# Gate/up groups of a hybrid decoder layer: the second weight block added by transfers onto two others, products in another order, and k tiles 8 to 11 by seven products

## The chip, the cores and the metric

The kernel runs on one core of one Trainium2 chip. The metric is the device time of one execution in microseconds (us); three runs of the kernel before have a median of 1966.47 us (1966.36 to 1967.82).

## The reference

One decoder layer on 256 tokens with D_MODEL 2048 and D_FF 5632, all in float32: a SwiGLU feed-forward half step with LayerNorm, a token mixer (latent attention beside differential attention, merged by sigmoid gates) with LayerNorm, and a second feed-forward half step with LayerNorm.

```python
def _swiglu(x, w_gate, w_up, w_down):
    return (jax.nn.silu(x @ w_gate) * (x @ w_up)) @ w_down

def reference(...):
    h = _layer_norm(ALPHA * h + 0.5 * _swiglu(h, ffn1_w_gate[l], ffn1_w_up[l], ffn1_w_down[l]), ...)
    mix = _mixer(h, ...)          # h @ w_in, two attentions, gates, w_out
    h = _layer_norm(ALPHA * h + mix, ...)
    h = _layer_norm(ALPHA * h + 0.5 * _swiglu(h, ffn2_w_gate[l], ffn2_w_up[l], ffn2_w_down[l]), ...)
```

## The kernel before

**Products in three parts.** Every float32 matmul is made of three matmuls on rounded operands (`triple`, L207 to L210): high part of x by high part of the weight (L208), high by low (L209), low by high (L210). A weight tile must therefore be split on the core first (`split`, L152 to L156): ScalarE (ACT) casts the raw tile to its high part (L154), VectorE (DVE) subtracts that from the raw tile to make the low part (L155). Both parts go into a ring of six pairs, `wring`.

**Units.** Work on weights is cut into units of two k tiles (a k tile is 128 rows of the weight) by 512 columns, one 128x1024 tile of 512 KB. `advance` (L173) runs three stages per unit in program order: `load` (a transfer issued by SP, three units ahead), `prep` (adds and split, four units ahead of the products) and `now` (the matmuls). A plain unit serves both blocks of 128 tokens: 2 k tiles x 2 token blocks x 3 = 12 matmuls of 512 columns.

**Gate/up by seven products.** `Hybrid.group` (L383 on) takes two neighbouring 512-column weights w0 and w1 together. For the k tiles that it handles this way the weight is a 2 by 2 matrix of blocks, "11" and "21" from w0, "12" and "22" from w1 (upper and lower k tiles), and the tokens' matrix is one of 2 by 2 blocks as well, so seven products do in place of eight (Strassen's scheme, in the form of Winograd). Products 1, 5, 6, 7, 2, 4, 3 run on sums of blocks: 1 on 11; 5 on 11+12; 6 on 11+12+22; 7 on 12+22; 2 on 21; 4 on 11+12+22+21; 3 on 22. The sums are made in place in the raw tiles `R[...]` before they are split. The tokens' sums are made once per layer part (`Seven` for k tiles 0 to 7, `Extra` for the others). The remaining k tiles are plain units, `p` on w0 and `q` on w1. PSUM banks X, Y, Z and W gather the products, and `done` subtracts or adds saved copies (`snaps`) and applies SwiGLU (gus L940, hb L921; transposed at L717 and sent out in 8 transfers at L719).

Each feed-forward part has a first pair of weights by `project` and ten groups, p = 1 to 10. Groups 2 to 9 are wide: their seven products cover k tiles 0 to 7 in two 128x1024 tiles per block (s = 0, 1) and k tiles 8 and 9 in one 128x512 tile per block (s = 2, `eraw`); k tiles 10 to 15 are three plain units on each weight. So a wide group has 7 x (6 + 6 + 3) = 105 matmuls by seven products and 6 x 12 = 72 plain ones, 177 in all. Groups 1 and 10 and six groups of the mixer (three for gates, wdq, wdk, wdv) are narrow: two tiles per block and 4 + 4 plain units.

**What sets the order.** The order of a group is a string, one character per product or plain unit: "15pp6p72q4q3q" for a wide group. Every engine executes its instructions in the order in which they were recorded, and `split_in_line` and `behind_split` tie the order of splits and adds on DVE. In a wide group three of the four sums are made by DVE (L430: 11 += 12 before product 5, 11 += 22 before 6, 11 += 21 before 4, each two adds of 128x1024 and one of 128x512). The fourth, 12 += 22 for product 7, is made by transfers that POOL issues (L432): each reads block 22 from memory once more and accumulates it onto 12 in place. In the mixer's groups DVE makes all four.

The blocks are loaded at L422, the plain units at L459.

## Time and profile before

| | |
|---|---|
| median of three runs | 1966.47 us (1966.36 to 1967.82) |
| the profiled execution, first to last instruction | 1963.9 us |
| what lies around that span, against the median | 2.6 us |
| TensorE (PE) busy | 1952.0 us, 99% |
| DVE busy | 1779.9 us, 91% |
| ACT busy | 1251.5 us, 64% |
| POOL busy | 312.1 us, 16% |
| mean granted TensorE clock | 0.998 |

The profile is of one execution. Its page gives busy times, the chain of work that ended last, groups of instructions and transfers; its trace answers for stretches of time, for the instructions of one engine in order of time, and for what an engine waited for. Busy times of neighbouring instructions on one engine overlap by some tens of ns, so the pitch from one start to the next says more than a duration.

### The profile page before, as it was taken

To read this page: it belongs to the slowest core of one execution; us is meant where nothing else is said; L and a number is where in the kernel's file an instruction comes from. 1 tells how busy PE (TensorE), PEld (TensorE's weight loads), DVE (VectorE), ACT (ScalarE), POOL (GpSimd) and SP (SyncE) were. 2 spreads that over 40 slices of the span, in tenths; PEclk is the share of its full clock that TensorE was granted. 3 is DMA by queue.
4 is the path that set the end of the run, shared out by engine and by line. 5 is a ranking of instruction groups with operands and counts; after the bars stand their busy time and mean duration, and the time that the engine had idled before them with its cause. 6 is when DMAs were issued, how large, how long until landed. Compare 5 with 4: busy or idle time off the path is not lost.

```text
span 1963.9 us, 25802 instructions
## 1 busy us (share of the span) xinstructions
PE 1952.0 (99%) x8763; PEld 1617.7 (82%) x8763; DVE 1779.9 (91%) x2189; ACT 1251.5 (64%) x1640; POOL 312.1 (16%) x536
## 2 busy tenths in 40 slices
PE   9999999999999999999999999999999999999998
PEld 7888888888888898888788888888888888888886
DVE  7999999999998879988987777789999999999997
ACT  6666766676655566666667655556676666665662
POOL 0112111122100010102241530001211112210000
PEclk9999999999999999999999999999999999999999
DMA  8978888878776667767685798587888878787773
GB/s 314 289 225 262 270 260 249 257 233 300 272 235 222 210 216 258 239 223 252 211 254 195 237 305 271 201 264 254 252 269 263 250 240 277 241 318 236 277 232 124
DMA packets 150228, 488.86 MB, mean 249 GB/s; under 512 B 21792, under 2 KB 22096, under 8 KB 150096
## 3 DMA queue, kind: packets, MB, share of 16 engines
q1 hardware_dynamic: 119232, 401.00, 59.7%
q0 software_dynamic: 30720, 86.09, 16.8%
q8 instruction: 68, 1.11, 0.2%
q14 instruction: 64, 0.52, 0.1%
q10 hardware_dynamic: 144, 0.13, 0.0%
HBM read 456.73 MB, written 30.41 MB: 248 GB/s over the span
## 4 chain that ended last, share of the span: by engine, by line
PE 95%; DVE 2%; DMA 1%; issue 1%; ACT 0%; POOL 0%; SPq 0%; DVEq 0%; ACTq 0%; POOLq 0%
PE mm L208 30%; PE mm L210 30%; PE mm L209 30%; DVE wring L155 1%; PE tr L208 1%; PE tr L210 1%; PE tr L209 1%; PE tr L673 0%; DMA turned<-turn 0%; ACT wring L154 0%; DMA sraw<-in_wdk_dram 0%; DVE sraw L430 0%; PE tr L1376 0%; PE tr L1304 0%; PE tr L1378 0%
## 5 line engine op out<-in xcount | busy, mean ns | idle before, releaser
L154 ACT CAST wring<-raw 128x1024 fp32r<-128x1024 f32 (+2 forms) x468 | 482.7, 1035 | 323.5 <-PE mm L210 237.6
L155 DVE TENSOR_TENSOR wring<-raw,wring 128x1024 fp32r<-128x1024 f32 (+2 forms) x468 | 557.0, 1198 | 95.6 <-ACT wring L154 93.5
L154 ACT CAST wring<-sraw 128x1024 fp32r<-128x1024 f32 x436 | 453.1, 1052 | 201.7 <-DVE sraw L430 83.6
L155 DVE TENSOR_TENSOR wring<-sraw,wring 128x1024 fp32r<-128x1024 f32 x436 | 520.3, 1218 | 20.6 <-ACT wring L154 17.8
L208 PE MATMUL mm<-wring,h 128*128 128x512 f32 (+2 forms) x1248 | 480.9, 385 | 0.1
L210 PE MATMUL mm<-wring,h 128*128 128x512 f32 (+2 forms) x1248 | 480.3, 385 | 0.0
L209 PE MATMUL mm<-wring,h 128*128 128x512 f32 (+2 forms) x1248 | 479.9, 385 | 0.0
L208 PE MATMUL mm<-wring,xs 128*128 128x512 f32 x776 | 302.2, 389 | 0.5 <-ACT snap L387 0.5
L209 PE MATMUL mm<-wring,xs 128*128 128x512 f32 x776 | 302.1, 389 | 0.0
L210 PE MATMUL mm<-wring,xs 128*128 128x512 f32 x776 | 301.9, 389 | 0.0
L210 PEld LDWEIGHTS mm<-wring,h 128*128 128x128 f32 x1248 | 234.4, 188 | 47.0 <-DVE h L155 0.7
L208 PEld LDWEIGHTS mm<-wring,h 128*128 128x128 f32 x1248 | 234.4, 188 | 46.7 <-ACT h L154 0.6
L209 PEld LDWEIGHTS mm<-wring,h 128*128 128x128 f32 x1248 | 234.4, 188 | 46.1
L430 DVE TENSOR_TENSOR sraw<-sraw,sraw 128x1024 f32<-128x1024 f32 x168 | 199.1, 1217 | 2.0 <-DMA sraw<-in_wdk_dram 1.6
L208 PEld LDWEIGHTS mm<-wring,xs 128*128 128x128 f32 x776 | 145.6, 188 | 31.0 <-ACT snap L387 0.9
L209 PEld LDWEIGHTS mm<-wring,xs 128*128 128x128 f32 x776 | 145.7, 188 | 30.5 <-DVE wring L155 0.3
L210 PEld LDWEIGHTS mm<-wring,xs 128*128 128x128 f32 x776 | 145.7, 188 | 30.2
L719 POOL DMA_DIRECT2D hT<-blocks x176 | 96.8, 563 | 368.3 <-DVE blocks L717 367.2
L209 PE MATMUL mm<-wring,x 128*128 128x512 f32 x336 | 130.9, 390 | 0.2 <-DVE wring L155 0.2
L208 PE MATMUL mm<-wring,x 128*128 128x512 f32 x336 | 130.1, 390 | 0.8 <-ACT wring L154 0.8
L210 PE MATMUL mm<-wring,x 128*128 128x512 f32 x336 | 130.7, 389 | 0.0
L432 POOL DMA_DIRECT2D sraw<-in_gu_dram x40 | 35.6, 892 | 371.4 <-DVE sraw L430 334.5
(328 smaller groups left out, 2292.4 us busy)
## 6 DMA issues: line engine op xcount, KB each, us to landing
sraw<-in_gu_dram SPq DMA_DIRECT2D x160, 512.0 KB, 5.2
raw<-in_gu_dram SPq DMA_DIRECT2D x158, 512.0 KB, 5.0
raw<-in_dn_dram SPq DMA_DIRECT2D x140, 512.0 KB, 4.7
sraw<-in_gu_dram POOLq DMA_DIRECT2D x40, 512.0 KB, 7.5
sraw<-in_dn_dram SPq DMA_DIRECT2D x36, 512.0 KB, 5.4
eraw<-in_gu_dram SPq DMA_DIRECT2D x64, 256.0 KB, 5.8
raw<-in_w_out_dram SPq DMA_DIRECT2D x32, 512.0 KB, 4.3
hraw<-hT POOLq DMA_DIRECT2D x56, 256.0 KB, 5.9
```

Source lines behind the costliest of these rows:

```text
L154: cast[0] = S.copy(hi, src)
L155: lows[0] = V.tensor_tensor(out=lo, in0=src, in1=hi.bitcast(F32), op=ALU.subtract)
L208: PE.matmul(o, xh, wh, start=first, stop=False, skip_group_check=again)
L209: PE.matmul(o, xh, wl, start=False, stop=False, skip_group_check=again)
L210: PE.matmul(o, xl, wh, start=False, stop=last, skip_group_check=again)
L430: last = V.tensor_tensor(out=R[src][i], in0=R[src][i], in1=R[add[1]][i], op=ALU.add)
L432: nc.gpsimd.dma_start(R["12"][s], source("22", s), accum_op=ALU.add)
L719: nc.gpsimd.dma_start(to.rearrange("(g r) (i f) -> i r g f", g=4, i=4)[i], t[32 * i:32 * (i + 1), :].rearrange("r (g f) -> r g f", g=4))
```

## The change

Block 12 is not loaded by itself any more. In every group transfers issued by POOL read it from memory and accumulate it in place onto block 11, once product 1 has been split from that, and onto block 22, once product 6's sum has been made from it (`added = {1: "11", 6: "22"}`, L436). DVE keeps two sums of each group: 11 += 22 for product 6 (L431), and 21 += 11 for product 4 (L439), made right behind the split of product 2 from the same tile.

The order of products changes to "15p36p27qn4q" for a wide group, and `Hybrid.run` records all groups of a part as one sequence: at the character n it emits product 1 of the next group, ahead of this group's product 4 and last q.

`Extra` now takes k tiles 8 to 11 by seven products (full 128x1024 tiles with s = 2), so a wide group has two plain units p and two q: 7 x 18 + 4 x 12 = 174 matmuls. Bank Z comes from the other PSUM pool. Lines move: the loads stand at L423 and L463, gus at L944, hb at L925, the transpose at L721 and its transfers at L723.

```diff
-            f = tmp_tile([P, 2, 2, P], "fe")
-            fa, fb = f[:, 0], f[:, 1]
+            a0, a1, c0, c1 = (raw[:, b, i * 256:(i + 1) * 256] for i in range(2) for b in range(2))
+            fa, fb = (tmp_tile([P, 2, 256], "fe") for _ in range(2))
             for out, in0, in1 in ((fa[:, 0], a1, c1), (fb[:, 0], a1, a0), (fa[:, 1], a0, fa[:, 0]), (fb[:, 1], c0, fa[:, 1])):
                 V.tensor_tensor(out=out, in0=in0, in1=in1, op=ALU.subtract)
-            t = act_tile([P, 2, 2, 2, P], F32R, "xe")
...
                 for m, p in enumerate(pair):
-                    self.at_[p] = [t[:, w, i, m] for w in range(2)]
-            k = 4 * self.q
+                    self.at_[p] = [t[:, w, m].rearrange("p (k t) -> p k t", k=2) for w in range(2)]
             for b, p in enumerate((2, 4)):
-                self.at_[p] = [self.x.at(w, k + 1, b) for w in range(2)]
...
@@ -356,22 +355,27 @@
...
             self.raws = {n: early[n] if n in early else [act_tile([P, 1024], F32, "sraw") for _ in range(2)]
-                         for n in ("11", "12", "22")}
-            self.raws["21"] = [act_tile([P, 1024], F32, "sraw") for _ in range(2)]
-            self.shared = False
+                         for n in ("11", "22", "21")}
             if extra is not None:
-                for pair in (("11", "12"), ("22", "21")):
-                    t = act_tile([P, 2, 512], F32, "eraw")
-                    for i, n in enumerate(pair):
-                        self.raws[n] = self.raws[n] + [t[:, i, :]]
+                for n in self.raws:
+                    self.raws[n] = self.raws[n] + [act_tile([P, 1024], F32, "sraw")]
...
+        def run(self, groups):
+
+            parts = [self.group(*g[:-1]) for g in groups]
+            for i, (order, emit) in enumerate(parts):
+                if groups[i][-1] is not None:
+                    groups[i][-1]()
+                for c in order if i == 0 else order[1:]:
+                    if c != "n":
+                        emit(c)
+                    elif i + 1 < len(parts):
+                        parts[i + 1][1]("1")
...
@@ -381,9 +385,10 @@
...
-            plan = {1: ("11", "11", None, "X"), 5: ("12", "11", ("11", "12"), "Z"), 6: ("22", "11", ("11", "22"), "X"),
-                    7: (None, "12", ("12", "22"), "X"), 2: ("21", "21", None, "Y"), 4: (None, "11", ("11", "21"), "W"),
-                    3: (None, "22", None, "Z")}
+            plan = {1: ("11", "11", None, "X"), 5: (None, "11", None, "Z"), 3: ("22", "22", None, "Z"),
+                    6: (None, "11", "22", "X"), 7: (None, "22", None, "X"), 2: ("21", "21", None, "Y"),
+                    4: (None, "21", None, "W")}
+            added = {1: "11", 6: "22"}
...
-                    banks[n] = mm_bank()
+                    banks[n] = tr_bank() if n == "Z" else mm_bank()
...
@@ -406,15 +411,11 @@
 
             def source(name, s):
                 w, j0 = blocks[name]
-                if s < 2:
-                    return w[j0 + s]
-                i = j0 // 2
-                return w[4][:, i * 512:(i + 1) * 512]
+                return w[j0 + s if s < 2 else 4 + j0 // 2]
...
                     last = None
-                    if add is not None and (small or p != 7):
+                    if add is not None:
                         for i in {0: (0,), 1: tuple(range(1, end_s + 1)), 2: ()}[s]:
                             with nullcontext() if small else behind_split(s + 1):
-                                last = V.tensor_tensor(out=R[src][i], in0=R[src][i], in1=R[add[1]][i], op=ALU.add)
-                    if not small and p == 6:
-                        nc.gpsimd.dma_start(R["12"][s], source("22", s), accum_op=ALU.add)
-                    pair = [v[:, :tiles * 512] for v in next_pair()]
+                                last = V.tensor_tensor(out=R[src][i], in0=R[src][i], in1=R[add][i], op=ALU.add)
+                    pair = next_pair()
                     with tc.issue_after(last.ins) if last is not None and not small else nullcontext():
                         split_in_line(not small, *pair, t)
-                    st["pair"] = [v.rearrange("p (g n) -> p g n", g=tiles) for v in pair]
+                    if p in added:
+                        nc.gpsimd.dma_start(R[added[p]][s], source("12", s), accum_op=ALU.add)
+                    elif p == 2:
+                        with nullcontext() if small else behind_split(1):
+                            V.tensor_tensor(out=t, in0=t, in1=R["11"][s], op=ALU.add)
+                    st["pair"] = [v.rearrange("p (g n) -> p g n", g=G) for v in pair]
...
-                    for g in range(tiles):
+                    for g in range(G):
                         if s < 2:
                             xh, xl = (v[:, 2 * s + g, :] for v in self.seven.at_[p])
                         else:
-                            xh, xl = self.extra.at_[p]
+                            xh, xl = (v[:, g, :] for v in self.extra.at_[p])
...
             end = self.k_tiles // G - 1
-            if self.shared:
-                order = "15pp6p7p3q2q4qq" if seeded else "1p5p6p7p3q2q4qq"
-            elif wide:
-                order = "15pp6p72q4q3q"
-            elif seeded:
-                order = "15pp6p7p2q4q3qq"
-            else:
-                order = "1p5p6p7p2q4q3qq"
-            turn = {n: iter(range(5 if wide else 4, end + 1)) for n in range(2)}
-            for i, c in enumerate(order):
-                if c in "pq":
-                    plain("pq".index(c), next(turn["pq".index(c)]), i == len(order) - 1)
+            order = "15p36p27qn4q" if wide else "1p5p36pp27qn4qqq" if self.begun else "1ppp5p3627qn4qqq"
+            self.begun = True
+            turn = {n: iter(range(6 if wide else 4, end + 1)) for n in range(2)}
+            left = [order.count("q")]
+
+            def emit(c):
+                if c == "p":
+                    plain(0, next(turn[0]))
+                elif c == "q":
+                    left[0] -= 1
+                    plain(1, next(turn[1]), left[0] == 0)
                 else:
                     for s in range(end_s + 1):
                         seventh(int(c), s)
+            return order, emit
...
-                name, w, j0 = (("11", 2, 0), ("12", 3, 0), ("22", 3, 2))[j // 2]
+                name, w, j0 = (("11", 2, 0), ("22", 3, 2), ("21", 2, 2))[j // 2]
...
+        hy.run([(wgu[2 * p], wgu[2 * p + 1],
+                 lambda n, b, bank, snap, op, p=p: sum_done(2 * p + n, b, bank, snap, op),
+                 1 < p < KF // 4 - 1, p > 1, False, ask if p == KF // 4 - 1 else None)
+                for p in range(1, KF // 4)])
```

First place, DVE between products 1 and 5 of a wide group, before. Tiles sraw_463, sraw_464 and eraw_471 hold block 11 (s = 0, 1, 2), sraw_465 and 466 block 12; L155 is the split's subtraction, L430 an add in place.

```order
L155 TENSOR_TENSOR wring_105<-sraw_463,wring_104 128x1024
L155 TENSOR_TENSOR wring_103<-sraw_464,wring_102 128x1024
L155 TENSOR_TENSOR wring_121<-eraw_471,wring_120 128x512
L430 TENSOR_TENSOR sraw_463<-sraw_463,sraw_465 128x1024
L430 TENSOR_TENSOR sraw_464<-sraw_464,sraw_466 128x1024
L940 TENSOR_TENSOR gus_2631<-mm_2367,snap_473 128x512
L155 TENSOR_TENSOR wring_119<-sraw_463,wring_118 128x1024
L940 TENSOR_TENSOR gus_2635<-mm_2340,snap_474 128x512
L921 TENSOR_TENSOR hb_2528<-gus_2631,sg_2633 128x256
L430 TENSOR_TENSOR eraw_471<-eraw_471 128x512
L155 TENSOR_TENSOR wring_117<-sraw_464,wring_116 128x1024
```

Product 5 follows product 1 directly; the adds between them are DVE's own.

The same place now. Here sraw_467, sraw_468 and sraw_473 hold block 11, sraw_471, 472 and 475 block 21 with the sum for product 4.

```order
L155 TENSOR_TENSOR wring_103<-sraw_467,wring_102 128x1024
L155 TENSOR_TENSOR wring_121<-sraw_468,wring_120 128x1024
L155 TENSOR_TENSOR wring_119<-sraw_473,wring_118 128x1024
L155 TENSOR_TENSOR wring_117<-sraw_471,wring_116 128x1024
L155 TENSOR_TENSOR wring_115<-sraw_472,wring_114 128x1024
L155 TENSOR_TENSOR wring_105<-sraw_475,wring_104 128x1024
L155 TENSOR_TENSOR wring_103<-raw_2192,wring_102 128x1024
L155 TENSOR_TENSOR wring_121<-sraw_467,wring_120 128x1024
L155 TENSOR_TENSOR wring_119<-sraw_468,wring_118 128x1024
L155 TENSOR_TENSOR wring_117<-sraw_473,wring_116 128x1024
L944 TENSOR_TENSOR gus_2263<-mm_2039,snap_476 128x512
```

Product 1 of the next group stands in the first three rows and its product 5 in rows 8 to 10, on the same three tiles; between them stand the three splits of product 4 and one of the last q.

Second place, POOL's queue in a wide group, before (hT is where the transposed SwiGLU results go, eight transfers in two rows):

```order
L432 DMA sraw_465<-in_gu_dram 128x1024
L432 DMA sraw_466<-in_gu_dram 128x1024
L432 DMA eraw_471<-in_gu_dram 128x512
L719 DMA hT_122<-blocks_3064 32x4x128 x4
L719 DMA hT_122<-blocks_3070 32x4x128 x4
```

and now, where sraw_469, sraw_470 and sraw_474 hold block 22:

```order
L436 DMA sraw_467<-in_gu_dram 128x1024
L436 DMA sraw_468<-in_gu_dram 128x1024
L436 DMA sraw_473<-in_gu_dram 128x1024
L436 DMA sraw_469<-in_gu_dram 128x1024
L436 DMA sraw_470<-in_gu_dram 128x1024
L436 DMA sraw_474<-in_gu_dram 128x1024
L723 DMA hT_122<-blocks_1828 32x4x128 x4
L723 DMA hT_122<-blocks_1834 32x4x128 x4
```

Six accumulating transfers of 512 KB take the place of two of 512 KB and one of 256 KB; those onto block 11 stand right behind the eight hT transfers of the group before.

More of the change, by code (lines that the diff above doesn't have):

```diff
@@ L416, in seventh @@
                 st = {}
-                tiles = G if s < 2 else 1
                 def load():
@@ L1256, in mixer, with room @@
         hy = Hybrid(x, seven, KD, True)
+        pairs = []
         for i, f in ((0, 0), (1, 0), (0, 2)):
             w = (a["wgm"], a["wgd"])[i]
-            hy.group(w[f], w[f + 1], lambda n, b, bank, snap, op, i=i, f=f: keep_gate(i, f + n, b, bank, snap, op),
-                     False, f == 2, True)
+            pairs.append((w[f], w[f + 1], lambda n, b, bank, snap, op, i=i, f=f: keep_gate(i, f + n, b, bank, snap, op),
+                          False, f == 2, True, None))
         def pair_cols(w, name):
-            dst = [act_tile([P, 4, T], F32, name) for _ in range(2)]
+            dst = []
+            def room():
+                dst.extend(act_tile([P, 4, T], F32, name) for _ in range(2))
             def done(n, b, bank, snap, op):
@@ L1268, in done @@
                 later(1, lambda: turn_to_cols(t, dst[n], b, 4, 10))
-            hy.group(w[0], w[1], done, False, True)
+            pairs.append((w[0], w[1], done, False, True, False, room))
             return dst
-        hy.share()
         dqT = pair_cols(a["wdq"], "dqT")
         dkT = pair_cols(a["wdk"], "dkT")
-        dv = [act_tile([P, 1024], F32, "dv") for _ in range(2)]
+        dv = []
         back = {}
@@ L1281, in c_back, with dv_room @@
                 nc.gpsimd.dma_start(back[key], src)
-        later(6, c_back)
-        for i in range(2):
-            for b in range(2):
-                later(12 + 4 * i + 2 * b, lambda i=i, b=b: cn.put(i, b, turned(back[i, b])))
-        hy.group(a["wdv"][0], a["wdv"][1], lambda n, b, bank, snap, op: whole(
-            dv[b][:, n * 512:(n + 1) * 512], bank, snap, op), False, True)
+        def dv_room():
+            dv.extend(act_tile([P, 1024], F32, "dv") for _ in range(2))
+            later(6, c_back)
+            for i in range(2):
+                for b in range(2):
+                    later(12 + 4 * i + 2 * b, lambda i=i, b=b: cn.put(i, b, turned(back[i, b])))
+        pairs.append((a["wdv"][0], a["wdv"][1], lambda n, b, bank, snap, op: whole(
+            dv[b][:, n * 512:(n + 1) * 512], bank, snap, op), False, True, False, dv_room))
+        hy.run(pairs)
         look(0, 0)
```

34 lines of the change are left out of this document (15 added, 19 removed).

## The prediction

> **What bounds the kernel now.** I read the page first: busy shares and the chain of work that ended last.
>
> ```profile
> span 1963.9 us, 25802 instructions
> PE 1952.0 (99%) x8763; PEld 1617.7 (82%) x8763; DVE 1779.9 (91%) x2189; ACT 1251.5 (64%) x1640; POOL 312.1 (16%) x536
> PE 95%; DVE 2%; DMA 1%; issue 1%; ACT 0%; POOL 0%; SPq 0%; DVEq 0%; ACTq 0%; POOLq 0%
> L154 ACT CAST wring<-sraw 128x1024 fp32r<-128x1024 f32 x436 | 453.1, 1052 | 201.7 <-DVE sraw L430 83.6
> L432 POOL DMA_DIRECT2D sraw<-in_gu_dram x40 | 35.6, 892 | 371.4 <-DVE sraw L430 334.5
> sraw<-in_gu_dram SPq DMA_DIRECT2D x160, 512.0 KB, 5.2
> sraw<-in_gu_dram POOLq DMA_DIRECT2D x40, 512.0 KB, 7.5
> ```
>
> PE carries 95% of the chain, so by itself a matmul less is time less. But DVE at 91% is an average; the wide groups must be read apart. The table of stretches: PE, PEld, DVE, ACT, POOL busy, clock, DMA share, GB/s. The first two lie in wide groups, the third around the narrow group 1 and the first wide ones, the last in the mixer.
>
> ```profile
> 200.00:250.00 50.00, 50.00 (x222) 41.40 (x221) 49.83 (x56) 32.62 (x42) 7.03 (x11) 1.00 0.86 268
> 250.00:300.00 50.00, 50.00 (x222) 41.41 (x221) 49.84 (x58) 34.04 (x45) 9.65 (x14) 1.00 0.87 249
> 40.00:90.00 50.00, 50.00 (x223) 41.39 (x222) 43.03 (x43) 30.39 (x35) 8.30 (x13) 1.00 0.94 326
> 950.00:1000.00 50.00, 49.49 (x222) 40.63 (x221) 43.56 (x58) 34.48 (x48) 13.85 (x26) 1.00 0.69 221
> ```
>
> In wide groups PE and DVE are both full: 50.00 and 49.83 of 50. The waits of PE, whole run, show who gives way:
>
> ```profile
> PE mm L208 <- ACT wring L154: 0.8, 1, 0.8
> PE mm L208 <- ACT snap L387: 0.5, 1, 0.5
> ```
>
> PE practically never waits for a split there, so PE sets the pace and DVE keeps up with next to nothing in hand. How little, the order of time on DVE tells (start, duration, instruction, count), with one period from the add at 248.88 to the same add at 289.00:
>
> ```profile
> 239.93 1.22 DVE L155 TENSOR_TENSOR wring<-raw,wring 128x1024 fp32r<-128x1024 f32 x1
> 241.06 2.36 DVE L155 TENSOR_TENSOR wring<-sraw,wring 128x1024 fp32r<-128x1024 f32 x2
> 243.34 0.69 DVE L155 TENSOR_TENSOR wring<-eraw,wring 128x512 fp32r<-128x512 f32 x1
> 243.94 0.69 DVE L940 TENSOR_TENSOR gus<-mm,snap 128x512 f32<-128x512 f32 x1
> 245.67 0.42 DVE L921 TENSOR_TENSOR hb<-gus,sg 128x256 f32<-128x256 f32 x1
> 246.01 2.35 DVE L155 TENSOR_TENSOR wring<-sraw,wring 128x1024 fp32r<-128x1024 f32 x2
> 248.88 2.36 DVE L430 TENSOR_TENSOR sraw<-sraw,sraw 128x1024 f32<-128x1024 f32 x2
> ...
> 265.64 2.36 DVE L155 TENSOR_TENSOR wring<-sraw,wring 128x1024 fp32r<-128x1024 f32 x2
> ...
> 268.52 1.30 DVE L717 STREAM_TRANSPOSE blocks<-hb 128x512 f32<-128x512 f32 x2
> 269.74 2.32 DVE L155 TENSOR_TENSOR wring<-sraw,wring 128x1024 fp32r<-128x1024 f32 x2
> ...
> 289.00 1.22 DVE L430 TENSOR_TENSOR sraw<-sraw,sraw 128x1024 f32<-128x1024 f32 x1
> ```
>
> The period is 40.12 us for 177 matmuls, 0.2267 us each. Pitches on DVE, start to start: 128x1024 1.135 us (2.28 for two from 241.06, 1.13 from 239.93), 128x512 0.60 (243.34 to 243.94), 128x256 0.335 (245.67 to 246.01), two transposes 1.22. A wide group has 20 splits and 6 adds of 128x1024, 13 operations of 128x512 (7 splits, 3 adds, 3 gus), two transposes and four hb: 26 x 1.135 + 13 x 0.60 + 1.22 + 4 x 0.335 = 39.87 us. DVE's slack is 0.25 us per group. Any wait put into DVE's row there lengthens the group.
>
> **The change, part by part: the two ledgers.** PE: 174 matmuls x 0.2267 = 39.44 us per wide group, 0.68 less; over 16 wide groups (8 in each feed-forward part) 48 x 0.2267 = 10.9 us. DVE now: 21 splits of sevenths, 4 plain ones and 6 adds of 128x1024, 3 gus, 2 transposes, 4 hb: 31 x 1.135 + 3 x 0.60 + 1.22 + 4 x 0.335 = 39.55 us. That is above PE's 39.44, so without any wait DVE would set 39.55 and a group would gain 0.57 us. ACT makes 25 casts of at most 1.05 us (page row, 1052 ns), 26 of 40 us: under DVE's full row it is hidden and costs nothing; without that cover it would still be 13 us short of the bound.
>
> **The new wait.** The sum 11 + 12 leaves DVE's ledger and becomes transfers. Each starts when product 1's split has read its tile, and product 5's cast and split of that tile wait for its landing. DVE executes in order, so behind a late product 5 everything queues: p, the SwiGLU steps, products 3, 6, 2, 7, and PE behind them, which has no other prepared units than the four ahead. The cover is what stands between: three splits of product 4 and one of q, 4 x 1.135 = 4.54 us. Transfers of this kind and their issue are in the trace, by start on POOL, and one by one with landing time:
>
> ```profile
> 210.28 0.93 POOL L432 DMA_DIRECT2D sraw<-in_gu_dram  x1 [16.59 <-DVE sraw L430]
> 211.41 0.86 POOL L432 DMA_DIRECT2D sraw<-in_gu_dram  x1 [0.21 <-issue]
> 250.41 0.91 POOL L432 DMA_DIRECT2D sraw<-in_gu_dram  x1 [16.60 <-DVE sraw L430]
> 269.52 4.41 POOL L719 DMA_DIRECT2D hT<-blocks  x8 [13.87 <-DVE blocks L717]
> ```
>
> ```profile
> L432 POOL DMA_DIRECT2D sraw<-in_gu_dram x1: 925/925/925, 210.3 to 210.3; - x1
> DMA to landing us min/median/max: 5.6/5.6/5.6
> ...
> L432 POOL DMA_DIRECT2D sraw<-in_gu_dram x1: 857/857/857, 211.4 to 211.4; - x1
> DMA to landing us min/median/max: 7.0/7.0/7.0
> ...
> L432 POOL DMA_DIRECT2D sraw<-in_gu_dram x1: 907/907/907, 250.4 to 250.4; - x1
> DMA to landing us min/median/max: 7.7/7.7/7.7
> ...
> L432 POOL DMA_DIRECT2D sraw<-in_gu_dram x1: 867/867/867, 251.5 to 251.5; - x1
> DMA to landing us min/median/max: 9.0/9.0/9.0
> ...
> L432 POOL DMA_DIRECT2D sraw<-in_gu_dram x1: 1023/1023/1023, 48.7 to 48.7; - x1
> DMA to landing us min/median/max: 9.1/9.1/9.1
> L432 POOL DMA_DIRECT2D sraw<-in_gu_dram x2: 863/943/1023, 48.7 to 49.9; - x2
> DMA to landing us min/median/max: 9.1/10.4/11.8
> ```
>
> The first of a pair lands 5.6 us after its issue and the second, issued 1.13 us later, at 211.41 + 7.0 = 218.4, which is 2.5 us after the first. The next group's pair, 250.41 + 7.7 and 251.5 + 9.0, is 2.4 us apart. They come out one behind the other, however closely they are issued. The issue follows the releasing DVE operation by 0.3 us (the add that starts at 248.88 takes 1.22 and the issue is at 250.41).
>
> Let product 1's first split start at 0. First issue 1.22 + 0.3 = 1.5; landings 7.1, 9.6 and, for a third tile, 12.1 (an estimate: one more step of 2.5). The cast, 1.05 us, comes before the split: with its handover 1.2. So the third split of product 5 can start at 13.3. In DVE's row it is due after 3 + 4 + 2 splits, at 9 x 1.135 = 10.2. DVE stands still for 3.1 us; the first tile alone would cost 8.3 - 7.95 = 0.35. The third tile decides.
>
> Before, the same kind of transfer (12 += 22) was issued at 250.41 and its tile split for product 7 at 265.64, 15 us later; this is why its 7.5 us on the page cost nothing. The bounds for the wait, s, per group: 3.1 with the 5.6 us row; 3.1 + 2.1 = 5.2 with the 7.7 us row; and in the crowded stretch 40 to 90 (first landing 9.1, the next 49.87 + 11.8 = 61.7, 3.8 behind it) 1.5 + 9.1 + 7.6 + 1.2 - 10.2 = 9.2. I weigh the first two alike: pairs of 5.6 and 7.0 and pairs of 7.7 and 9.0 in equal number have a median of 7.35, and the page has 7.5 for all 40. That makes s = 4.15, at a DMA share of 0.87.
>
> The share will not stay. Per wide group the transfers go from 16 plain tiles of 512 KB and 2.5 accumulating ones to 13 and 6. An accumulating one takes the 2.5 us; a plain one at 326 GB/s (stretch 40 to 90) 1.6 us: + 3.5 x 2.5 - 3 x 1.6 = +3.95 us on 0.865 x 40.12 = 34.7, so 38.65 us per group. Drawing a line between s = 4.15 at 0.87 and 9.2 at 0.94 (72 us per unit of share), and taking the share as 38.65 / (39.55 + s), the two meet near s = 4.5 (share 0.877, by the line 4.7). I take 4.5, an estimate.
>
> In a sentence by itself: the Trainium skill, page "DMA: Bandwidth & Descriptors", section "Anatomy of one DMA — SWDGE (gpsimd) path", gives a transfer issued by GpSimd 2.0 us and its bytes at 436 GB/s; that is 3.2 us for 512 KB, the third tile would land at 7.0, ahead of its use, and the sum would be the gain of 10.9. The trace disagrees with it for accumulating transfers: 5.6 us for the first and 2.5 for each behind it.
>
> **The other edits.** *Second accumulation* (12 onto 22, after product 6's adds, for product 7): between lie product 6, p, product 2 and its first adds, 11 operations or 12.5 us, against 0.3 + 9.1 + 1.2 at worst: nothing; without that cover the same wait again. *POOL's queue*: the eight hT issues take 4.41 us just ahead of the accumulations onto 11; DVE has the transposes, 3 splits, one hb and a split in that time, 6.2 us against 0.7 + 0.3 + 4.4: nothing, or some tenths. *Block 11's reload* waits for product 4's adds; its load (5.2 us) has about 2 us to spare. *Group 1*: product 5 behind "1ppp" waits up to 9 us, but the three p are 3 x 2.72 us for PE: 0 to 3 us per part, 2 us for both. *Mixer*: four adds less per group on DVE, but PE is busy 49.49 of 50 there, so a gain of at most 1.5 us, and a queue of POOL transfers ahead of two accumulations that DVE's slack covers: 0. *Reserve*: DVE's lead over PE at the start of the wide groups delays the first waits; I allow one split, 1.135 us, once per part (it could be up to four units of 1.36 us, 5.4 us); product 5 of group 2 has three q and a two-tile product 4 for cover, five splits in place of four, and comes out of a narrow group, so its wait goes into that lead.
>
> **Sum.** Groups 3 to 10 of each part take one wait each: 16 x (39.55 - 40.12) = -9.1; 16 x 4.5 = +72.0; reserve -2.3; group 1 +2. That makes +62.6 us, in general 16 s - 9.4. The sum is made against the profiled span 1963.9; the median, 1966.47, is 2.6 us longer, and the difference carries over: 1966.47 + 62.6 = 2029 us.
>
> **Rivals.** *The transfers are in time (A, the other side).* If the third accumulation lands within 7.5 us of the first issue in place of 10.6, because the 2.5 us spacing belongs to the traffic at that moment and not to the accumulation, s is under 0.2; PE sets the time and the change gives 10.9 us: 1955.6. For it: no stretch of before has three full accumulations in a row, and the pairs shown ran beside loads. Against: those pairs are 2.4, 2.5 and 3.8 us apart. 0.12. The page of the Trainium skill named above gives this case. *A part of the wait (B).* Fewer plain loads run beside the accumulations than in the pairs shown, the spacing falls to between 1.4 and 2.2 us, and s is 0.9 to 2.5: +5 to +31 us. The DMA share of 0.87 speaks against so quiet a stretch. 0.10. *Crowding (C).* Accumulations and the loads of block 21 and q push each other as in the first group, s from 6 to 9.2: +87 to +138, up to 2104. The share of 0.94 and the 9.1 us row speak for it; that it feeds back (a longer group has a lower share) against it. 0.09. *No difference to speak of (D)*: DVE's wait just pays for the matmuls saved, s near 0.6, or the edits do not act as read; 48 fewer matmuls stand in the order, so little for it. 0.03.
>
> **Numbers.** Forecast (s from 2.5 to 6: +31 to +87) 0.66. The range goes from s = 1.45, +14, 1980 us, to s = 7.4, +109, 2075 us; it leaves out A, D and the outer third of B and of C, about 0.2. A measurement can tell about 0.2%, 3.9 us, from no change. Faster: A, 0.12. Same: D and a little of B, 0.04. Slower: 0.84.
>
> **What would show it.** Accumulations at L436 one period apart with that period 43 to 45 us; DVE busy about 0.9 in wide groups and its splits L155 of sraw idle behind ACT's casts, those behind a transfer of in_gu_dram; PE waiting for wring some 4 us per group; the third transfer landing 10 to 12 us after the first issue. It is wrong if PE stays at 50.00 of 50 in those stretches, if the three land about 1.1 us apart, or if the idle time stands at product 7 or at block 11's reload.

## The result, and the profile after

The changed kernel takes 2109.45 us (median of 4 runs, 2107.79 to 2112.6) against 1966.51 for the kernel before in the same comparison: ratio 1.0729, 95% interval 1.0713 to 1.0745, 143 us slower. The forecast was 2029 with a range to 2075. The sign and the main place were right; the size was not.

The page of the profile after: span, busy times, the chain that ended last, the casts of block tiles, the accumulations onto blocks 11 and 22 (L436), and the time to landing of transfers issued by POOL.

```profile
span 2107.9 us, 25662 instructions
PE 2007.5 (95%) x8715; PEld 1626.6 (77%) x8715; DVE 1747.0 (83%) x2079; ACT 1269.4 (60%) x1610; POOL 381.4 (18%) x616
PE 30%; DVE 9%; DMA 6%; issue 4%; ACT 1%; POOL 1%; DVEq 0%; POOLq 0%; ACTq 0%
L154 ACT CAST wring<-sraw 128x1024 fp32r<-128x1024 f32 x548 | 567.1, 1049 | 406.5 <-DMA sraw<-in_gu_dram 174.6
L436 POOL DMA_DIRECT2D sraw<-in_gu_dram x112 | 96.9, 900 | 566.7 <-DVE sraw L431 430.5
sraw<-in_gu_dram POOLq DMA_DIRECT2D x112, 512.0 KB, 8.0
```

No engine is full any more: PE 95%, DVE 83%. The casts waited 174.6 us for transfers of gate/up blocks. Where in a group that lies, DVE's order of time shows; these are product 1 and product 4 (six splits from 225.26), q, then product 5's three splits, each with the idle time before it:

```profile
225.26 6.90 DVE L155 TENSOR_TENSOR wring<-sraw,wring 128x1024 fp32r<-128x1024 f32 x6
232.06 1.23 DVE L155 TENSOR_TENSOR wring<-raw,wring 128x1024 fp32r<-128x1024 f32 x1
235.67 1.23 DVE L155 TENSOR_TENSOR wring<-sraw,wring 128x1024 fp32r<-128x1024 f32 x1 [2.38 <-ACT wring L154]
239.48 1.22 DVE L155 TENSOR_TENSOR wring<-sraw,wring 128x1024 fp32r<-128x1024 f32 x1 [2.58 <-ACT wring L154]
243.33 1.22 DVE L155 TENSOR_TENSOR wring<-sraw,wring 128x1024 fp32r<-128x1024 f32 x1 [2.62 <-ACT wring L154]
```

The wait is where it was forecast, at product 5, and nowhere else in this group. It is 2.38 + 2.58 + 2.62 = 7.58 us, not 4.5. In the seven groups of the first feed-forward part that have all three waits, they add up to between 6.74 and 8.14 us. POOL's order of time gives the period, from the accumulations onto block 22 to the next such, and those onto block 11 between them:

```profile
206.19 0.85 POOL L436 DMA_DIRECT2D sraw<-in_gu_dram  x1 [23.81 <-DVE sraw L431]
...
227.05 1.80 POOL L436 DMA_DIRECT2D sraw<-in_gu_dram  x2 [1.31 <-ACT wring L154]
229.05 0.84 POOL L436 DMA_DIRECT2D sraw<-in_gu_dram  x1 [0.20 <-issue]
253.56 0.85 POOL L436 DMA_DIRECT2D sraw<-in_gu_dram  x1 [23.67 <-DVE sraw L431]
```

253.56 - 206.19 = 47.37 us per wide group against 40.12: 7.25 more, and 39.55 + 7.58 = 47.13 by the prediction's ledger. The time to landing of transfers of that group: the first and the third onto block 22, then onto block 11 the first, and the second and third in one row:

```profile
L436 POOL DMA_DIRECT2D sraw<-in_gu_dram x1: 848/848/848, 206.2 to 206.2; - x1
DMA to landing us min/median/max: 5.4/5.4/5.4
...
L436 POOL DMA_DIRECT2D sraw<-in_gu_dram x1: 848/848/848, 208.5 to 208.5; - x1
DMA to landing us min/median/max: 8.3/8.3/8.3
...
L436 POOL DMA_DIRECT2D sraw<-in_gu_dram x1: 909/909/909, 227.1 to 227.1; - x1
DMA to landing us min/median/max: 7.4/7.4/7.4
...
L436 POOL DMA_DIRECT2D sraw<-in_gu_dram x2: 842/887/932, 227.9 to 229.0; - x2
DMA to landing us min/median/max: 10.4/11.8/13.1
```

Onto block 22 the first lands at 211.6 and the third (issued at 208.5) at 216.8: two steps of 2.6 us in the mean, as before. Onto block 11 they land at 234.5, 238.3 and 242.1: 3.8 apart. What differs stands in SP's queue (L423 loads blocks, L463 plain units) and in the stretches, among them the one from issue to last landing:

```profile
225.05 0.33 SPq L463 DMA_DIRECT2D raw<-in_gu_dram  x1
229.95 2.56 SPq L423 DMA_DIRECT2D sraw<-in_gu_dram  x3
233.32 0.33 SPq L463 DMA_DIRECT2D raw<-in_gu_dram  x1
```

```profile
200.00:250.00 50.00, 44.57 (x183) 34.56 (x181) 42.42 (x44) 30.62 (x37) 9.58 (x14) 0.97 0.78 221
226.00:244.00 18.00, 16.73 (x72) 13.05 (x71) 10.42 (x10) 8.65 (x10) 2.64 (x3) 1.00 1.00 291
```

Three loads of block 21 and two of plain units are issued into the same 9 us. Over the whole group the DMA engines are less busy than before (0.78, before 0.86); from 226 to 244 they are full (1.00). But a full share does not tell the two places apart: the accumulations onto block 22 fill the engines too (1.04 to 1.06 in each 2 us from 210 to 216). What differs is whose transfers fill them. Here q0 is the queue of POOL's transfers and q1 that of SP's, each with packets, MB and its share of the engines' time, first from 206 to 218 (block 22), then from 226 to 244 (block 11):

```profile
q0 software_dynamic: 432, 1.57, 71.9%
q1 hardware_dynamic: 167, 0.62, 14.9%
...
q1 hardware_dynamic: 932, 3.37, 50.3%
q0 software_dynamic: 579, 1.86, 49.6%
```

The loads suffer as well: the three of block 21 take 8.6 to 11.3 us to land, where the page has a median of 5.9. They come just then because block 21's tiles become free by product 4's splits, the very splits that were to cover the wait.

### The profile page after: what moved, and what is told of

It reads as the page before. It is cut to its first block, busy times and chain, and to the rows that moved or that the text cites. A ratio compares the mean times of both kernels' runs of the same rounds, so it can differ in the third digit from the quotient of the medians.

```text
span 2107.9 us, 25662 instructions
## 1 busy us (share of the span) xinstructions
PE 2007.5 (95%) x8715; PEld 1626.6 (77%) x8715; DVE 1747.0 (83%) x2079; ACT 1269.4 (60%) x1610; POOL 381.4 (18%) x616
## 4 chain that ended last, share of the span: by engine, by line
PE 30%; DVE 9%; DMA 6%; issue 4%; ACT 1%; POOL 1%; DVEq 0%; POOLq 0%; ACTq 0%
PE mm L208 9%; PE mm L210 9%; PE mm L209 9%; DVE wring L155 5%; DMA sraw<-in_gu_dram 5%; PE tr L209 1%; PE tr L208 1%; PE tr L210 1%; DVE sraw L439 1%; DVE sraw L431 1%; DVE gus L944 1%; ACT wring L154 1%; DVE hb L925 1%; DVE blocks L721 1%; POOL sraw L436 0%
## 5 line engine op out<-in xcount | busy, mean ns | idle before, releaser
L154 ACT CAST wring<-sraw 128x1024 fp32r<-128x1024 f32 x548 | 567.1, 1049 | 406.5 <-DMA sraw<-in_gu_dram 174.6
L155 DVE TENSOR_TENSOR wring<-sraw,wring 128x1024 fp32r<-128x1024 f32 x548 | 651.8, 1220 | 179.7 <-ACT wring L154 177.6
L155 DVE TENSOR_TENSOR wring<-raw,wring 128x1024 fp32r<-128x1024 f32 (+2 forms) x436 | 519.2, 1198 | 104.8 <-ACT wring L154 102.8
L208 PE MATMUL mm<-wring,h 128*128 128x512 f32 (+2 forms) x1104 | 428.7, 388 | 7.8 <-ACT snap L393 7.7
L209 PE MATMUL mm<-wring,h 128*128 128x512 f32 (+2 forms) x1104 | 427.2, 387 | 0.4
L210 PE MATMUL mm<-wring,h 128*128 128x512 f32 (+2 forms) x1104 | 427.0, 387 | 0.0
L209 PE MATMUL mm<-wring,xs 128*128 128x512 f32 x568 | 231.8, 408 | 30.2 <-DVE wring L155 30.2
L208 PEld LDWEIGHTS mm<-wring,h 128*128 128x128 f32 x1104 | 209.0, 189 | 53.0 <-ACT snap L393 12.2
L209 PEld LDWEIGHTS mm<-wring,h 128*128 128x128 f32 x1104 | 208.8, 189 | 43.1 <-DVE wring L155 2.8
L210 PEld LDWEIGHTS mm<-wring,h 128*128 128x128 f32 x1104 | 208.8, 189 | 41.2 <-DVE h L155 0.7
L208 PE MATMUL mm<-wring,xs 128*128 128x512 f32 x568 | 229.8, 405 | 2.0 <-ACT wring L154 1.9
L210 PE MATMUL mm<-wring,xs 128*128 128x512 f32 x568 | 229.5, 404 | 0.0
L436 POOL DMA_DIRECT2D sraw<-in_gu_dram x112 | 96.9, 900 | 566.7 <-DVE sraw L431 430.5
L209 PEld LDWEIGHTS mm<-wring,xs 128*128 128x128 f32 x568 | 111.2, 196 | 61.0 <-DVE wring L155 37.8
L723 POOL DMA_DIRECT2D hT<-blocks x176 | 96.9, 560 | 294.0 <-DVE blocks L721 292.7
L208 PEld LDWEIGHTS mm<-wring,xs 128*128 128x128 f32 x568 | 110.7, 195 | 29.8 <-ACT wring L154 6.6
L208 PE MATMUL tr<-wring,xs 128*128 128x512 f32 x280 | 112.8, 403 | 19.4 <-ACT snap L393 18.6
L210 PEld LDWEIGHTS mm<-wring,xs 128*128 128x128 f32 x568 | 111.4, 196 | 23.2
L209 PE MATMUL tr<-wring,xs 128*128 128x512 f32 x280 | 111.5, 398 | 2.1 <-DVE wring L155 1.9
L210 PE MATMUL tr<-wring,xs 128*128 128x512 f32 x280 | 111.0, 396 | 0.0
L208 PE MATMUL mm<-wring,x 128*128 128x512 f32 x240 | 93.6, 395 | 3.5 <-ACT snap L393 3.5
```

The costliest lines, as they stand in the source:

```text
L154: cast[0] = S.copy(hi, src)
L155: lows[0] = V.tensor_tensor(out=lo, in0=src, in1=hi.bitcast(F32), op=ALU.subtract)
L208: PE.matmul(o, xh, wh, start=first, stop=False, skip_group_check=again)
L209: PE.matmul(o, xh, wl, start=False, stop=False, skip_group_check=again)
L210: PE.matmul(o, xl, wh, start=False, stop=last, skip_group_check=again)
L436: nc.gpsimd.dma_start(R[added[p]][s], source("12", s), accum_op=ALU.add)
```

## The experiments

Theory: product 5 waits for the accumulations onto block 11, which share the DMA engines with block 21's reload; the cover in DVE's row is too short for that. Rivals: the accumulations are so slow by themselves; another wait stands behind this one; the part on k tiles 8 to 11 is what costs. Each ratio is to runs of the kernel before in the same comparison, whose medians were 1966.02, 1966.37 and 1966.09; the changed kernel's 2109.45 is from the comparison above.

**Block 21 held back.** Three one-column memsets on DVE after product 5 keep block 21's reload waiting until then.

```diff
+                    if p == 5 and s == end_s and seeded and not small:
+                        with behind_split(1):
+                            for held in R["21"]:
+                                V.memset(held[:, 0:1], 0.0)
```

> The changed kernel, except that in groups 2 to 10 of both feed-forward parts the reload of block 21 is held back until product 5 has been split (three one-column memsets on VectorE make it wait), so that it no longer runs beside the three accumulations onto block 11. Crowding theory (the accumulations land 3.8 us apart because loads of block 21 and q share the DMA engines with them): spacing falls to 2.6 to 3.0 us, the wait per group from 7.6 to 5.0 to 6.0, and the time from 2109 to 2065 to 2085. Own-pace theory (three accumulations in a row take 3.8 us each by themselves): spacing stays at 3.8, the time at 2105 to 2113.

Measured: 2082.62 us, ratio 1.0596 (1.0580 to 1.0612). DVE at product 5, and SP's loads of plain units ahead of it, in the kernel with block 21 held:

```profile
275.27 1.23 DVE L155 TENSOR_TENSOR wring<-sraw,wring 128x1024 fp32r<-128x1024 f32 x1 [2.04 <-ACT wring L154]
277.72 1.23 DVE L155 TENSOR_TENSOR wring<-sraw,wring 128x1024 fp32r<-128x1024 f32 x1 [1.23 <-ACT wring L154]
281.39 1.23 DVE L155 TENSOR_TENSOR wring<-sraw,wring 128x1024 fp32r<-128x1024 f32 x1 [2.45 <-ACT wring L154]
```

```profile
264.97 8.61 SPq L467 DMA_DIRECT2D raw<-in_gu_dram  x2
```

The first two splits are 2.45 us apart now, the last still 3.67; the wait is 5.72 us. As far as block 21 goes the crowding theory holds: 27 us come back when the same transfers are not accompanied by its loads. It is not the whole wait: the first accumulation still lands 7.1 us after its issue (7.4 with block 21 beside it), and only one of the two steps became shorter. A second plain unit's load, issued near 273, still runs beside the third accumulation. That this load is what spaces the third was not tried.

**Plain copies in place of accumulations onto block 11.** The transfers overwrite, so products 5, 6 and 4 work on other sums.

```diff
-                        nc.gpsimd.dma_start(R[added[p]][s], source("12", s), accum_op=ALU.add)
+                        nc.gpsimd.dma_start(R[added[p]][s], source("12", s), **({} if p == 1 else {"accum_op": ALU.add}))
```

> The changed kernel, except that the transfers of block 12 onto block 11 are plain copies (they overwrite; products 5, 6 and 4 then work on other sums); their number, bytes, queue and waits stay. If it is the accumulating that is slow: first landing about 5 us after its issue, 1.3 to 2 us between landings, a wait of 0 to 1.5 us per group, 1980 to 2015 us. If it is the bytes, or the issue by POOL: landings and time as before, 2100 to 2113.

Measured: 2015.0 us, ratio 1.0257 (1.0235 to 1.0278). DVE at product 5 with plain copies:

```profile
262.07 1.23 DVE L155 TENSOR_TENSOR wring<-sraw,wring 128x1024 fp32r<-128x1024 f32 x1 [0.36 <-ACT wring L154]
263.52 1.23 DVE L155 TENSOR_TENSOR wring<-sraw,wring 128x1024 fp32r<-128x1024 f32 x1 [0.22 <-ACT wring L154]
265.71 1.22 DVE L155 TENSOR_TENSOR wring<-sraw,wring 128x1024 fp32r<-128x1024 f32 x1 [0.97 <-ACT wring L154]
```

The wait is 1.55 us, just over the 1.5 of the expectation. The copies land 5.4 us, 5.6 and 7.1 after their issues (255.47, 256.60 and 257.46), so 1.3 and 2.4 us apart. With the same number, bytes of weight, queue and place, and block 21's loads beside them as before (issued from 258.36), 94 of the 143 us are gone. The engines are no less busy: their share is 1.00 from 254 to 267, but they move 395 GB/s there, where they moved 291 with accumulations. So an accumulation takes more of the engines' time than a copy of the same tile, and crowding costs this much only because of that.

**No transfers onto block 11.** Products 5, 6 and 4 work on sums without block 12.

```diff
-            added = {1: "11", 6: "22"}
+            added = {6: "22"}
```

> The changed kernel without the transfers of block 12 onto block 11 at all (products 5, 6 and 4 work on sums without block 12; the transfers onto block 22 stay). If the wait of product 5 is the whole loss of the wide groups: their period falls from 47.4 to 39.6 us and the time to 1965 to 1985, with the rest in the mixer. If another wait stands close behind it (block 11's reload, product 7, a PSUM bank): a period of 42 us or more, 2010 us or more.

Measured: 1978.39 us, ratio 1.0065 (1.0048 to 1.0082). POOL's accumulations onto block 22, one period apart:

```profile
265.80 0.91 POOL L436 DMA_DIRECT2D sraw<-in_gu_dram  x1 [20.12 <-DVE sraw L431]
...
305.54 0.92 POOL L436 DMA_DIRECT2D sraw<-in_gu_dram  x1 [20.23 <-DVE sraw L431]
```

39.74 us: DVE's ledger (39.55) sets the pace and no second wait stands behind the first. But 12 us above the kernel before remain, with groups 0.4 us shorter than before; they lie outside the wide groups.

**The mixer as before.** The six mixer groups with blocks 12 loaded and four sums on DVE, by the old class beside the new one. The old class brings its own order of products and its own buffers with it, so this takes back the whole change in the mixer, not its transfers alone.

```diff
-        hy = Hybrid(x, seven, KD, True)
+        hy = HybridB(x, seven, KD, True)
```

> The changed kernel with the mixer's six groups as they were before (blocks 12 loaded, four sums on VectorE, no transfers of POOL there). If the 22 us that the mixer lost come from its own accumulations: 2084 to 2092 us. If they come from what the first feed-forward part leaves behind: 2104 to 2113.

Measured: 2091.62 us, ratio 1.0635 (1.0615 to 1.0655): 18 us come back between the medians. The traces say 22: from SP's first plain load of the gates' weights to its first load behind the six groups (L236) it is 278.7 us in the kernel before, 300.9 in the changed one and 277.7 with the mixer as before. A slow stretch of the mixer in the changed kernel, and the same stretch of time with the mixer as before:

```profile
1000.00:1020.00 20.00, 17.52 (x57) 13.03 (x58) 13.33 (x13) 11.99 (x15) 5.08 (x8) 0.74 0.89 275
```

```profile
1000.00:1020.00 20.00, 20.00 (x89) 16.35 (x88) 20.00 (x22) 15.49 (x20) 6.65 (x13) 1.00 0.64 203
```

PE issues 57 matmuls in place of 89; it is idle for 2.5 us, and its granted clock has a mean of 0.74.

**K tiles 8 to 11 alone**, in the kernel before: the new `Extra`, full tiles for s = 2, and one plain unit less on each weight.

```diff
-                tiles = G if s < 2 else 1
+                tiles = G
...
-                order = "15pp6p72q4q3q"
+                order = "15p6p72q43q"
...
-            turn = {n: iter(range(5 if wide else 4, end + 1)) for n in range(2)}
+            turn = {n: iter(range(6 if wide else 4, end + 1)) for n in range(2)}
```

> The kernel before with one part of the change alone: k tiles 8 to 11 by seven products (174 matmuls per wide group, one plain unit less on each weight), with the blocks, sums and order of before. If VectorE's ledger sets the time: 34 x 1.135 + 3 x 0.60 + 1.22 + 4 x 0.335 = 42.95 us per wide group, +2.83 against before, 2011 us (2003 to 2019). If TensorE set it: 16 x 3 matmuls less, 1955 to 1960.

Measured: 2018.97 us, ratio 1.0273 (1.0250 to 1.0295). The accumulations, one period apart, in that kernel:

```profile
219.07 0.93 POOL L426 DMA_DIRECT2D sraw<-in_gu_dram  x1 [17.30 <-DVE sraw L424]
...
262.44 0.91 POOL L426 DMA_DIRECT2D sraw<-in_gu_dram  x1 [17.18 <-DVE sraw L424]
```

43.37 us, the ledger said 42.95. DVE sets the time; three matmuls fewer bring nothing while DVE makes nine adds a group. This is why this part of the change needs the transfers.

**Two sets of tiles for block 11.** Product 1 of the next group no longer needs this group's block 11 to be finished, and moves ahead of products 2 and 7.

```diff
+                self.other = [act_tile([P, 1024], F32, "sraw") for _ in range(3)]
...
-            R = self.raws
+            R = dict(self.raws)
+            self.raws["11"], self.other = self.other, self.raws["11"]
...
-            order = "15p36p27qn4q" if wide else ...
+            order = "15p36pn27q4q" if wide else ...
```

> The changed kernel with two sets of tiles for block 11 in the feed-forward parts, so that product 1 of the next group can be split before products 2 and 7 of this one (order 15p36pn27q4q): 14 operations of VectorE in place of 4 stand between product 1 and product 5, the transfers are the same. If the short cover is the cause: no wait at product 5, wide groups of 39.6 us, 1985 to 2005 us (the mixer and group 1 stay slow). If the DMA engines can't carry the six accumulations and 13 loads in 39.6 us: periods of 42 us or more, with the wait at another tile, 2030 us or more.

Measured: 1996.54 us, ratio 1.0156 (1.0140 to 1.0171). A stretch of wide groups, and POOL's accumulations onto block 22:

```profile
200.00:250.00 50.00, 50.00 (x222) 41.26 (x221) 50.00 (x50) 37.57 (x44) 13.50 (x21) 1.00 0.93 264
```

```profile
228.06 0.92 POOL L440 DMA_DIRECT2D sraw<-in_gu_dram  x1 [16.55 <-DVE sraw L435]
...
267.58 0.92 POOL L440 DMA_DIRECT2D sraw<-in_gu_dram  x1 [16.90 <-DVE sraw L435]
```

39.52 us per group with every transfer and every product kept. PE and DVE are full, and the DMA engines carry it at a share of 0.93. The transfers themselves are hardly faster: those onto block 11, issued at 235.73, 236.87 and 238.00, land 7.4, 9.2 and 11.9 us later, the last 14.2 us after the first issue (15.1 in the changed kernel). What takes the wait away is the cover: that it was too short for these landings was the cause.

**The transfers without k tiles 8 to 11**: the old `Extra` and half tiles for s = 2, in the changed kernel.

```diff
+                tiles = G if s < 2 else 1
...
-            order = "15p36p27qn4q" if wide else ...
+            order = "15pp36p27qqn4q" if wide else ...
```

> The changed kernel without its part on k tiles 8 to 11: half tiles for s = 2 and three plain units on each weight as before (177 matmuls), with the transfers and the new order (15pp36p27qqn4q). VectorE's ledger without a wait is 37.0 us, so 3.1 us of a wait are free. If the wait with landings 3.8 us apart is about 6 us: periods of 42.5 to 44 us, 2025 to 2055 us with what the mixer and group 1 lose. If half a third tile brings it under 3.1 us: 40.1 us, 1990 to 2005 us.

Measured: 2063.61 us, ratio 1.0504 (1.0484 to 1.0523), 9 us above the range of the expectation. DVE in that kernel, the last q and product 5:

```profile
222.04 1.23 DVE L155 TENSOR_TENSOR wring<-raw,wring 128x1024 fp32r<-128x1024 f32 x1 [1.41 <-ACT wring L154]
225.55 1.22 DVE L155 TENSOR_TENSOR wring<-sraw,wring 128x1024 fp32r<-128x1024 f32 x1 [2.28 <-ACT wring L154]
229.35 1.22 DVE L155 TENSOR_TENSOR wring<-sraw,wring 128x1024 fp32r<-128x1024 f32 x1 [2.58 <-ACT wring L154]
231.38 0.69 DVE L155 TENSOR_TENSOR wring<-eraw,wring 128x512 fp32r<-128x512 f32 x1 [0.80 <-ACT wring L154]
```

In this group the wait is 5.66 us at product 5, as forecast, and 1.41 more at the q ahead of it, which was not; the four periods from 197.28 to 377.07 have a mean of 44.95 us, above the forecast 42.5 to 44. So without k tiles 8 to 11 the change still loses 97 of the 143 us, with what mixer and group 1 lose in it. The part on k tiles 8 to 11 adds the other 46, though it takes PE's work away: by the ledgers it fills the 3.1 us that DVE would have had free, and it makes the third transfer a full one.

**Two sets and the mixer as before**: both edits above together, nothing else.

> Two sets of tiles for block 11 and the longer cover, and the mixer's groups as they were before: the change without its two losses. If those are the whole of it apart from group 1: 1966 to 1980 us. If the cover doesn't remove the wait: 2010 us or more.

Measured: 1977.79 us, ratio 1.0057 (1.0042 to 1.0072): the mixer gives 18.75 us once more (1996.54 to 1977.79).

**Group 1 as before, besides.** With two sets and the old mixer, group 1 of each part gets back the plan, the order of products and the early loads that it had; block 12 uses the second set of tiles.

```diff
+            lone = not self.begun and not small
+            if lone:
+                R["12"] = self.raws["11"]
+                plan = {1: ("11", "11", None, "X"), 5: ("12", "11", "12", "Z"), 6: ("22", "11", "22", "X"),
...
+                added = {}
...
+                    if lone and p == 6:
+                        nc.gpsimd.dma_start(R["12"][s], source("22", s), accum_op=ALU.add)
```

> Two sets of tiles for block 11, the longer cover and the mixer as before, and group 1 of each feed-forward part with the plan and the early loads that it had before (sums by VectorE; block 12 in the second set of tiles). With two sets and the mixer as before alone the time was 1977.8 us, 11.4 above the kernel before, though the wide groups ran at 39.5 us in place of 40.12. If group 1's own waits are what is left (4 to 6 us and a lower clock in each part): 1958 to 1966 us. If the loss lies in the token sums or at the ends of the parts: 1974 us or more.

Measured: 1960.55 us (8 runs, 1960.13 to 1963.48), ratio 0.9975 (0.9965 to 0.9985) to the kernel before. Its busy times:

```profile
PE 1944.4 (99%) x8715; PEld 1607.9 (82%) x8715; DVE 1771.6 (90%) x2107; ACT 1278.5 (65%) x1610; POOL 356.6 (18%) x588
```

Group 1's new plan cost 17.2 us in all between the medians (1977.79 to 1960.55; 13.4 between the two profiled executions), and without it this version is 5.5 us faster than the kernel before: little, but the interval of the ratio leaves out 1. The ledger allows 16 x (40.12 - 39.55) = 9.1. Not all of the 17.2 was seen as waits: with two sets and the mixer as before, PE waits 4.3 us from 20 to 130 and 3.7 from 1330 to 1450, around the two groups 1, where it waits for nothing in the kernel before; its clock is 0.91 from 80 to 100.

**One split more of cover** in the changed kernel, by moving n ahead of the q.

```diff
-            order = "15p36p27qn4q" if wide else ...
+            order = "15p36p27n4qq" if wide else ...
```

> The changed kernel with one character of the wide order moved (15p36p27n4qq): five splits stand between product 1 and product 5 in place of four, transfers as they are. If the wait is landing time less cover: each group is 1.1 us shorter, 16 to 18 us in all, 2088 to 2096 us. If the earlier product 1 then waits for block 11's reload, or landings are as much later: 2104 us or more.

Measured: 2080.91 us, ratio 1.0582 (1.0567 to 1.0596), 28.5 us less, where 16 to 18 were expected, and 7 us below the range. DVE at product 5 with one more split ahead:

```profile
229.91 1.23 DVE L155 TENSOR_TENSOR wring<-sraw,wring 128x1024 fp32r<-128x1024 f32 x1 [1.31 <-ACT wring L154]
233.69 1.23 DVE L155 TENSOR_TENSOR wring<-sraw,wring 128x1024 fp32r<-128x1024 f32 x1 [2.56 <-ACT wring L154]
234.84 0.68 DVE L944 TENSOR_TENSOR gus<-mm,snap 128x512 f32<-128x512 f32 x1
237.47 1.23 DVE L155 TENSOR_TENSOR wring<-sraw,wring 128x1024 fp32r<-128x1024 f32 x1 [1.95 <-ACT wring L154]
```

The first wait is 1.07 us shorter, as one split more should make it, and the last 0.67, because a gus operation now runs inside the wait. That makes the 1.8 us per group.

## Why the prediction was wrong

**The ledgers held.** DVE's 39.55 us was measured as 39.52 where nothing waits, and 42.95 as 43.37 for the other ledger. By the prediction's own sum, 16 s - 9.4, an s of 7.58 gives +112 us for the two feed-forward parts; by SP's loads in the two traces these parts lost 64.6 us (up to the first plain load of the mixer's gates, 725.1 before and 789.7 now) and 56.9 (from the first load behind the six groups, 1003.8 and 1090.6, to the last of the down-projection, 1930.5 and 2074.2), 121.5 in all.

**The wait was found, its size was not.** Cover, cast and order were as worked out, and the first issue came only 0.3 us later than the 1.5 taken: 1.5 + 7.4 + 2 x 3.8 + 1.2 - 10.2 = 7.5 with the measured landings. The first landing, 7.4, lies between the two rows taken (5.6 and 7.7, in the mean 6.65) and adds 0.75 us. The term that was mis-sized is the spacing: 3.8 us for 2.5, twice, or 2.6 of the 3.35 us between 4.15 and 7.5. The third accumulation landed 15.1 us after the first issue, where 10 to 12 were forecast.

The step that failed is the one that was to price crowding: "Drawing a line between s = 4.15 at 0.87 and 9.2 at 0.94", with the share taken "as 38.65 / (39.55 + s)". It went by the mean DMA share over a group. That mean did fall, to 0.78, and the spacing still rose to 3.8, since block 21's loads and the accumulations meet in the same 18 us. I had counted product 4's splits as cover and not asked what they set free. The right row was in the prediction's own list: the pair issued at 48.7 also landed 3.8 us apart. SP's queue had 55.0% of the engines' time from 48 to 62 there, against 20.4% from 210 to 218.5 and 27.7% from 250 to 260.5, where the pairs landed 2.5 and 2.4 apart; in the changed kernel 14.9% goes with 2.6 and 50.3% with 3.8. Five windows are no law, but they order by what SP's queue takes, which the total share doesn't do. Rival C named the mechanism, "Accumulations and the loads of block 21 and q push each other", with +87 to +138; the argument that it feeds back, by which it got 0.09, was the same mean.

**The rival of transfers in time** is out: the first accumulation onto block 22 took 5.4 us, and the two steps behind it 2.6 in the mean, even where SP's queue took 14.9% of the engines' time. The section of the Trainium skill that gave that case has no term for the accumulating. Another section of the same page ("DMA: Bandwidth & Descriptors", section "Queues, rings and completion order") says that each DMA engine takes turns between the queues that have work for it; the trace agrees with that, with 49.6% of the engines' time for POOL's queue and 50.3% for SP's from 226 to 244.

**Two terms were put at next to nothing.** The mixer was put at 0 ("a queue of POOL transfers ahead of two accumulations that DVE's slack covers"); it cost 18 us by two pairs of kernels, 22 by the traces. Group 1 was put at 2 for both parts; it cost 17.2, measured in kernels whose wide groups don't wait.

The wide groups must be summed from all of them, not from the one shown. In each part seven periods hold the whole wait; by POOL's accumulations onto block 22 they are 49.6 us longer than before in the first part (111.02 to 443.62, before 87.77 to 370.76) and 47.2 in the second, 6.9 each. The eighth, into the narrow group 10, is longer by 2.9 and 1.4. That makes 101 us, where the prediction had 72.0 - 9.1 = 63. Wide groups 101, group 1 17 and mixer 22 are 140 of the 144 us between the two profiled executions; the rest stays open, and so does whether group 1 costs the same ahead of a waiting DVE as ahead of a full one.

## What to carry to other kernels

When the work that is to cover a transfer also frees buffers, the reloads start in that very window: list what each covering instruction releases, not only how long it takes, and read who uses the DMA engines in that window, not their share over the period. DVE had no slack here, and a wait of 7.58 us made a group of 39.55 us one of 47.37; so a transfer whose landing is uncertain by some microseconds wants a cover of the longest landing seen. A second set of tiles bought 10 more operations of cover, and turned 7% slower into the version that, with mixer and group 1 as before, is 0.25% faster.

## What was not expected of the hardware

Accumulating transfers of 512 KB onto block 22 landed 2.6 us apart; plain copies from the same queue, with block 21's loads beside them, landed 1.3 and 2.4 us apart. With a full DMA share in both cases, 395 GB/s were moved with copies onto block 11 and 291 with accumulations.

Where PE had waited, its granted clock was lower for a while: 0.97 over the wide groups of the changed kernel, 0.74 in one stretch of its mixer, 1.00 in the same stretch without the waits. In steps of 2 us these means come apart: the clock is 0.50 from 1002 to 1012 in the mixer and from 210 to 212 in a wide group, and back at 1.00 from 1012 and from 214. The Trainium skill, page "TensorE: Matmul & The Clock Gate", section "HAM oscillation — how this bites in real kernels", describes a clock that falls to half when PE stands idle for more than about 3.4 us. The rows agree with the half, but not with the length: the longest single wait of PE ahead of these two places was 1.4 and 1.8 us, with several short ones close together. Near 1037, with a wait of 4.3 us and a clock of 0.50 behind it, it is as the page has it. The prediction had given all this no price. In the wide groups, where DVE sets the time, the period of 47.37 us is only 0.24 longer than ledger and wait together, so it costs no more than that there; what part it has in the mixer's loss was not separated.
